# Three unsorted experts, the last gate/up products ahead of the last down products, and a later read of half the scattered rows

## The chip, the cores and the metric

The kernel runs on one core of one Trainium2 chip, as one launch. The metric is the device time in microseconds (us) of one execution. Engines are named as the profile names them: PE is TensorE (PEld its weight loads), DVE is VectorE, ACT is ScalarE, POOL is GpSimd, SP is SyncE, which here only issues transfers. Each engine works through its own queue in order.

## The reference

Two blocks follow each other on 512 tokens of width 1024, in float32. The first has two layers of latent attention with convolution branches. The second has dilated and forgetting attention and then a mixture of 32 experts; only the experts and the last norm are touched here.

```python
group_logits = xt @ w_rg + b_rg                  # 4 groups: the best one is taken
expert_logits = (xt @ w_re + b_re)               # 8 experts in it: the best two are taken
expert_id = g_idx * EXPERTS_PER_GROUP + top_i    # two experts for each of 512 tokens
for e in range(N_EXPERTS):
    he = silu(xt @ w_gate[e]) * (xt @ w_up[e])   # 1024 -> 256
    y = y + combine[:, e:e + 1] * (he @ w_down[e])   # 256 -> 1024
x = x + y
return _rmsnorm(x, final_norm)
```

So there are 1024 pairs of a token and an expert, and 3 MiB of weights for each expert: 2 MiB of gate and up, 1 MiB of down.

## The kernel before, in words

The experts are worked off one after the other. `second_out` and `route_tile` compute the normed tokens, write them to DRAM (`h2d`), and find for each pair its expert and its rank in that expert. `tables_of` turns that into lists of token rows.

The first AH = 5 experts are taken in their natural order, with a block of 128 rows each. The other 27 are sorted by their number of rows (`sort_experts`), so that each place in the order has a fixed block size: `TIERS` gives the first three places of the sorted ones 128 rows, the next two 96, then 64, then 32. The order of work is the string `SEQ`: f stands for the next sorted expert with over 64 rows, m for one with 64, s for one with 32. What doesn't fit into a block goes to extra blocks (`route_extra`, and the loop in `overflow` at the end, which runs as often as there are such blocks). The addresses of a sorted expert's weights come from registers of SP, loaded at L1960 out of the sorted order.

Each expert goes through these steps. `gather` fetches its token rows with an indirect transfer (L1810). `ex_turn` transposes them on PE (`pturn`). `gu` forms the gate and up products (`pgu`): L1827 for blocks over 64 rows, L1838 for small ones, which `fold` then turns and sums (`pfold`, `ef`). `ex_act` forms the gated activation (`eh`). The down products follow in one of two ways. A block over 64 rows has `pye` (L1866), is scaled, and `scatter` writes its rows into a buffer in DRAM (`yd`, one row for each pair) with an indirect transfer. Small blocks go two by two through `pair`: `pyf` (L1887), split in two float32r parts (L1894, L1896), and when 128 rows are together, `ex_add` spreads them over all tokens with a selecting product (`psel`) and adds them to `xk` (L1916). `back` reads the scattered rows (`yb`, L2045) and adds them to `xk` (L2048).

`step(e)` issues the loads ahead (`load`: gate and up of expert e + 5, down of e + 3), the gate/up products of e + 1, the down products of e, the turn of e + 2, the gather of e + 4, some waiting adds, and the fold of e + 1. PE's order is that of the code (`manual_schedule`); a planner orders the other engines' work within the dependences. Gate and up weights lie in a ring of 16 tiles of 512 KB (`eraw`) and four more (`wraw`, for every fifth expert); the reads of scattered rows (`yb`) take tiles of the same ring. Down weights have four places (`wh`, `wl`). All their loads, the reads of `yb` and the writes of the output are in SP's queue. Before the sort, `route_end` issues gate and up of experts 2 to 4 (0 and 1 come earlier), and the down weights of the first three; the fourth's need no sorted order either.

`finish` goes over the four row tiles: the last adds, a square with its sum on ACT (L1928), a root by ten small DVE operations (`rsq`, L231 to L240) for the tiles that `FT` names, the scaling (L1936) and the write of the output (L1937).

Of the kernel before, what the change touches and what calls it, by code (L numbers as in the profile page):

```python
# [10 lines left out]
F32 = mybir.dt.float32  # L11
# [4 lines left out]
OP = mybir.AluOpType  # L16
# [8 lines left out]
NE = 32  # L25
# [4 lines left out]
UNIT = 1040  # L30
PTC = 2
PS2 = (3, 2, 2)
FT = ((0, 2, 1), (2, 4, 3))
HB = 2


# [49 lines left out]
FF = (0.3, 0.2, 0.3)  # L86
PTB = 3
FA, FB = 1.2, 2.4
AH = 5
WH = 3  # L90
TIERS = ((3, 128), (5, 96), (15, 64), (32, 32))
NX = 16
SX = 10
SB = 3
YB = 6
R3 = 0
EL = 3
SO = ((0, 0, 0, 1, 1, 1, 0, 2, 2, 2, 1, 0), (3, 0, 3, 1, 3, 2, 3, 1, 2, 3, 2, 3))
RB = 22
SEQ = "ssfmmfssfmmfssfmmssmmssmmss"  # L100
BE = (lambda nc: nc.vector, lambda nc: nc.vector)
LWP = 8
SQ = "n0 n1 n2 v m2 t0 m2 t1 m2 t2 m2 c0 h00 s2 b04 h10 m2 b04 h20 m2 b14 m4 c1 h01 b14 s2"
# [7 lines left out]
class K:  # L111
# [1741 lines left out]
    def ex_act(self, p, mp):  # L1853

        nc = self.nc
        h = mp.tile([128, 2, 128], F32, name="eh", tag="eh", bufs=3)[:, :, :p.shape[3]]
        nc.scalar.activation(h, p[:, 0], AF.Tanh, scale=0.5)
        nc.vector.scalar_tensor_tensor(h, h, 1.0, p[:, 0], op0=OP.add, op1=OP.mult)
        nc.vector.tensor_tensor(h, p[:, 1], h, op=OP.mult)
        return h  # L1860
# [57 lines left out]
    def finish(self, add):  # L1918
# [5 lines left out]
        for t in range(4):  # L1924
# [4 lines left out]
            os.append(o)  # L1929
            for a, b, at in FT:  # L1930
                if at != t:
# [7 lines left out]
    def moe(self):  # L1939
        nc, I, sp, tc = self.nc, self.I, self.sp, self.tc  # L1940
        xk = self.xk
        mp = self.pool("moe")
# [4 lines left out]
        U, Dn, X, Hs, at = dict(enumerate(self.ahead)), dict(enumerate(self.wd)), {}, {}, {}  # L1947
# [6 lines left out]
        def w_of(i, e):  # L1954
            e = cols[e]
            if e < AH:
                return ws[i][e]
            if e not in at:
                j = e - AH
                at[e] = nc.values_load(self.order[0:1, j:j + 1], engines=[mybir.EngineType.SP], min_val=AH, max_val=NE - 1)  # L1960
            return ws[i][bass.ds(at[e], 1)].rearrange("o a b -> (o a) b")
# [2 lines left out]
            return a[:, cols[e]:cols[e] + 1]  # L1964

        def load(e):
            if e + AH < NE:
                U[e + AH] = self.ex_load(e + AH, w_of(0, e + AH), w_of(1, e + AH))
            if e + WH < NE:
                Dn[e + WH] = self.ex_wd(w_of(2, e + WH))  # L1970

# [4 lines left out]
        def turn(e):  # L1976
            if e < NE:
                X[e] = self.ex_turn(xgs[e % 2], mp, cap[e], e < 2)
# [6 lines left out]
        nc.gpsimd.iota(self.io512, pattern=[[1, 512]], base=0, channel_multiplier=0, allow_small_or_imprecise_dtypes=True)  # L1985
        with tc.issue_after(self.tabled.ins):
            self.sort_experts(mp)
        G = {}

        def gu(e):  # L1990
            if cap[e] > 64:
                Hs[e] = self.ex_gu(U[e], X[e], mp)
            else:
                G[e] = self.ex_half(U[e], X[e], mp, cap[e])

        def fold(e):
            if cap[e] <= 64:
                Hs[e] = self.ex_fold(G[e], mp, cap[e])

# [6 lines left out]
            sc.append(st)  # L2006


        nm, ns = 5, 3
        by = mp.tile([128, 2, nm + ns], F32, name="by")  # L2010

        def rows_by():
            for x, a in enumerate((self.tok, self.wsl)):
                for i in range(2):
                    nc.vector.tensor_copy(by[64 * i:64 * i + 64, x, :nm], a[:64, SX + i:SX + 2 * nm:2])
                for i in range(4):
                    nc.vector.tensor_copy(by[32 * i:32 * i + 32, x, nm:], a[:32, SX + 2 * nm + i:NE:4])

# [19 lines left out]
        B = {}  # L2038

        def back(t):  # L2040

            if t < 4:
                for k in range(2):
                    y = B[t, k] = self.eraw("yb")
                    nc.sync.dma_start(y, self.yd[k * 512 + t * 128:k * 512 + t * 128 + 128, :])  # L2045
            for k in range(2):
                if t:
                    BE[k](nc).tensor_tensor(xk[:, t - 1, :], xk[:, t - 1, :], B[t - 1, k], op=OP.add)  # L2048

        gu(0)  # L2050
        turn(1)
# [3 lines left out]
        waiting, full = [], None  # L2055

        def add(n):

            for x in waiting[:n]:
                self.ex_add(*x)  # L2060
            del waiting[:n]

        def step(e):
            nonlocal full
            load(e)
            if e + 1 < NE:
                gu(e + 1)
            full = None
            if cap[e] > 64:
                scatter(e)  # L2070
            elif cap[:e + 1].count(cap[e]) % 2 == 0:
                full = pair(e)
            turn(e + 2)
            gather(e + 4)
            add(2 if cap[min(e + 1, NE - 1)] > 32 else 1)
            if e + 1 < NE:
                fold(e + 1)
            if e == 1:
                self.route_extra(mp)
                rows_by()  # L2080
            if RB <= e <= RB + 4:
                back(e - RB)
            if full and e + 1 < NE:
                waiting.extend(full + (t,) for t in range(4))

        for e in range(3):
            step(e)
        with tc.manual_schedule(engines={mybir.EngineType.PE}):
            for e in range(3, NE):
                step(e)  # L2090
            add(4)
        self.finish(lambda t: self.ex_add(*full, t))
        self.overflow(mp, xgs[0])
        mp.release()
        self.rp.release()
# [70 lines left out]
```

## Time and profile before

| | us |
|---|---|
| median of 3 runs | 1437.74 (1432.52 to 1438.69) |
| the profiled execution | 1439.8 |
| its span, first to last instruction | 1437.7 |
| PE busy in the span | 1315.5 (92%) |
| DVE busy | 951.7 (66%) |
| ACT busy | 610.1 (42%) |
| POOL busy | 313.4 (22%) |

The mean transfer rate over the span is 171 GB/s. Busy shares are means over stages of different kinds, so the rows below look at the last 340 us alone. In the table by stretches, "DMA share" is the mean busy share of the 16 DMA engines and "PEclk" the granted clock of TensorE, 1.00 being 2.4 GHz and 0.50 being 1.2 GHz. In a timeline, brackets give the idle time of the engine before an instruction and what ended it; instructions in DMA queues (SPq) are issues, not landings.

### The profile page before, as it was taken

What the parts mean: (1) busy time and instruction counts of PE and PEld (TensorE: products, weight loads), DVE (VectorE), ACT (ScalarE), POOL (GpSimd) and SP (SyncE); (2) the same over time, 40 slices, a digit from 0 to 9 for tenths busy, and PEclk for the clock granted to TensorE, in tenths of its full rate; (3) what the DMA queues carried; (4) which work ended last, traced back from release to release, by engine and by line L of the source; (5) the groups of instructions that cost most, each with busy time, mean ns of one, the idle gap of its engine ahead of it and who ended that gap; (6) DMA issues with size and microseconds to landing.
All of it is one profiled execution on the core that took longest, in us unless ns stands there. A gap on an engine that the chain in (4) does not pass through costs nothing. (4 is left out here: it accounts for less than half of the span.)

```text
span 1437.7 us, 22499 instructions
## 1 busy us (share of the span) xinstructions
PE 1315.5 (92%) x8030; PEld 1044.9 (73%) x8030; DVE 951.7 (66%) x2123; ACT 610.1 (42%) x1195; POOL 313.4 (22%) x414
## 2 busy tenths in 40 slices
PE   4999999989989999799999999999997999999873
PEld 3888788877868788678877787887776877675441
DVE  5789997666633789997683646666667443444555
ACT  4543264545531564266573336767553111112111
POOL 5332033322220333143231201111111121111100
PEclk9999999999999999999999999999997999999987
DMA  9643364444132435434233455224545699999971
GB/s 346 150 137 103 100 169 124 129 137 144 63 123 73 116 108 156 125 87 116 69 120 131 151 177 132 77 72 138 171 174 190 222 303 359 378 369 386 389 286 59
DMA packets 167317, 246.45 MB, mean 171 GB/s; under 512 B 47267, under 2 KB 103289, under 8 KB 167205
## 3 DMA queue, kind: packets, MB, share of 16 engines
q1 hardware_dynamic: 161116, 234.95, 49.7%
q0 software_dynamic: 5408, 7.93, 2.1%
q10 hardware_dynamic: 680, 2.13, 0.4%
q8 instruction: 64, 1.05, 0.3%
q14 instruction: 49, 0.39, 0.1%
HBM read 221.74 MB, written 33.33 MB: 177 GB/s over the span
## 5 line engine op out<-in xcount | busy, mean ns | idle before, releaser
L183 DVE TENSOR_TENSOR wlo<-wraw,whi 128x1024 fp32r<-128x1024 f32 (+3 forms) x98 | 118.2, 1212 | 59.3 <-ACT whi L182 58.7
L182 ACT ACTIVATE whi<-wraw 128x1024 fp32r<-128x1024 f32 (+3 forms) x98 | 100.6, 1036 | 102.0 <-PE pout L221 42.7
L219 PE MATMUL pcm<-hTh,whi 128*128 128x256 f32 (+1 forms) x288 | 102.9, 357 | 9.3 <-DVE oa L529 4.3
L569 DVE SCALAR_TENSOR_TENSOR za<-zp,vec,za 128x783 f32<-128x783 f32 (+1 forms) x120 | 108.8, 914 | 0.5
L921 POOL TENSOR_SCALAR P<-P,ll 128x768 f32<-128x768 f32 (+1 forms) x80 | 73.4, 922 | 159.8 <-DVE ll L920 144.9
L221 PE MATMUL pcm<-hTh,wlo 128*128 128x256 f32 (+1 forms) x288 | 99.1, 344 | 0.1
L220 PE MATMUL pcm<-hTl,whi 128*128 128x256 f32 (+1 forms) x288 | 98.6, 342 | 0.0
L183 DVE TENSOR_TENSOR PTl<-pPT,PTh 128x512 fp32r<-128x512 f32 x104 | 70.3, 684 | 28.2 <-ACT PTh L182 27.8
L182 ACT ACTIVATE PTh<-pPT 128x512 fp32r<-128x512 f32 x104 | 60.6, 595 | 47.6 <-PE pPT L934 43.4
L919 ACT ACTIVATE P<-pS,nm 128x768 f32<-128x768 f32 (+1 forms) x80 | 64.9, 814 | 37.4 <-DVE nm L917 31.1
L1810 POOL DMA_INDIRECT xg<-h2d,tok x32 | 31.5, 984 | 209.2 <-PE pturn L1794 131.2
L1416 POOL TENSOR_SCALAR P<-P,l 128x384 f32<-128x384 f32 (+1 forms) x64 | 33.2, 532 | 184.7 <-DVE l L1415 167.6
L917 DVE TENSOR_REDUCE nm<-pS 128x1 f32<-128x768 f32 (+1 forms) x80 | 66.0, 843 | 10.9 <-PE pS L221 10.2
L219 PEld LDWEIGHTS pcm<-hTh,whi 128*128 128x128 f32 x288 | 55.2, 192 | 17.5 <-DVE oa L529 4.9
L219 PE MATMUL pcm<-hT0h,whi 128*128 128x512 f32 x144 | 59.3, 412 | 7.7 <-DVE oa L529 5.8
L934 PE MATMUL pPT<-ident,P 128*128 128x128 f32 x416 | 63.3, 281 | 0.9 <-DVE PTl L183 0.4
L1827 PE MATMUL pgu<-exT,eraw 128*128 128x128 f32 x512 | 61.8, 281 | 0.0
L1827 PEld LDWEIGHTS pgu<-exT,eraw 128*128 128x128 f32 x512 | 60.3, 197 | 1.1 <-DVE exT L1805 0.6
L221 PEld LDWEIGHTS pcm<-hTh,wlo 128*128 128x128 f32 x288 | 55.1, 191 | 6.8 <-DVE wlo L183 0.8
L966 POOL TENSOR_TENSOR oa<-oa,ot 64x256 f32<-64x256 f32 x40 | 37.4, 936 | 102.6 <-DVE ot L965 99.3
L220 PEld LDWEIGHTS pcm<-hTl,whi 128*128 128x128 f32 x288 | 55.3, 192 | 5.1 <-issue 0.5
L220 PE MATMUL pcm<-hT0l,whi 128*128 128x512 f32 x144 | 58.4, 406 | 0.0
(552 smaller groups left out, 3681.6 us busy)
## 6 DMA issues: line engine op xcount, KB each, us to landing
wraw<-in_w_in_dram SPq DMA_DIRECT2D x56, 512.0 KB
eraw<-in_w_expert_gate_dram SPq DMA_DIRECT2D x52, 512.0 KB
eraw<-in_w_expert_up_dram SPq DMA_DIRECT2D x52, 512.0 KB
wraw<-in_w_mod_dram SPq DMA_DIRECT2D x48, 512.0 KB
wl<-in_w_expert_down_dram SPq DMA_DIRECT2D x32, 512.0 KB
wh<-in_w_expert_down_dram SPq DMA_DIRECT2D x32, 512.0 KB
wraw<-in_w_out_dram SPq DMA_DIRECT2D x24, 512.0 KB
wraw<-in_w_expert_gate_dram SPq DMA_DIRECT2D x12, 512.0 KB
```

What stands on the lines that cost most here:

```text
L182: nc.scalar.activation(hi, src, AF.Copy)
L183: return (eng or nc.vector).tensor_tensor(lo, src, hi.bitcast(F32), op=OP.subtract)
L219: mm(out, lhs[0], rhs[0], start=start, stop=False)
L220: mm(out, lhs[0], rhs[1], start=False, stop=False)
L221: mm(out, lhs[1], rhs[0], start=False, stop=stop)
L569: nc.vector.scalar_tensor_tensor(a[:, :nz], z[:, k:k + nz], cfw[:, i, k:k + 1], a[:, :nz], op0=OP.mult, op1=OP.add)
L917: nc.vector.tensor_reduce(nm, S, axis=AX.X, op=OP.max, negate=True)
L919: nc.scalar.activation(P, S, AF.Exp, bias=nm, accum_out=l)
L921: nc.gpsimd.tensor_scalar(P, P, l, 0.5, op0=OP.mult, op1=OP.mult)
L934: nc.tensor.transpose(p[:, jj, i * 128:(i + 1) * 128], Ps[i][:, (j + jj) * 128:(j + jj + 1) * 128], self.ident)
L966: nc.gpsimd.tensor_tensor(o, o, t, op=OP.mult)
L1827: self.last = self.nc.tensor.matmul(p[:, s, c, :], gu[2 * s + k // 4][:, k % 4, c * 128:(c + 1) * 128], x[:, k, :], start=(k == 0), stop=( ...
```

## The change: what it does

- AH goes from 5 to 3: three unsorted experts, 29 sorted ones. The depth of the loads ahead stays at five (LA), so gate and up of the fourth and fifth expert are now loaded after the sort. The tiers become three of 128, two of 96, eight of 64 and sixteen of 32 among the sorted ones: 8 experts are scattered where 10 were, and there are 8 experts with 64 rows where 10 were, and 16 with 32 where 12 were.
- The gated activation has two buffers for blocks over 32 rows and four for those of 32, in place of three for all.
- `route_extra` moves from step 1 to step 15.
- The reads of scattered rows for the first two row tiles come at steps 20 and 21, with their adds a step later. Those for the last two are issued after the last down weights, and their adds stand in `finish`.
- Steps run to 27 only. Then come the gate/up products of the last three experts with their folds and the waiting adds, and after them the last two pairs of down products.
- `FT` names one root over all four row tiles, after the last one, in place of one for each two.

```diff
-FT = ((0, 2, 1), (2, 4, 3))
+FT = ((0, 4, 3),)
...
-AH = 5
+AH = 3
+LA = 5
 WH = 3
-TIERS = ((3, 128), (5, 96), (15, 64), (32, 32))
+TIERS = ((3, 128), (5, 96), (13, 64), (32, 32))
 NX = 16
-SX = 10
+SX = 8
...
-RB = 22
-SEQ = "ssfmmfssfmmfssfmmssmmssmmss"
+RB = 20
+END = 28
+SEQ = "ssfmmfssfmmfssfssmmssssmmssss"
...
-        h = mp.tile([128, 2, 128], F32, name="eh", tag="eh", bufs=3)[:, :, :p.shape[3]]
+        n = p.shape[3]
+        h = mp.tile([128, 2, 128 if n > 32 else n], F32, name="eh", tag=f"eh{n > 32}", bufs=2 if n > 32 else 4)[:, :, :n]
...
-            if e + AH < NE:
-                U[e + AH] = self.ex_load(e + AH, w_of(0, e + AH), w_of(1, e + AH))
+            if e + LA < NE:
+                U[e + LA] = self.ex_load(e + LA, w_of(0, e + LA), w_of(1, e + LA))
...
             self.sort_experts(mp)
+        for e in range(AH, LA):
+            U[e] = self.ex_load(e, w_of(0, e), w_of(1, e))
...
-        nm, ns = 5, 3
+        nm, ns = 4, 4
...
-            if t < 4:
-                for k in range(2):
-                    y = B[t, k] = self.eraw("yb")
-                    nc.sync.dma_start(y, self.yd[k * 512 + t * 128:k * 512 + t * 128 + 128, :])
             for k in range(2):
-                if t:
-                    BE[k](nc).tensor_tensor(xk[:, t - 1, :], xk[:, t - 1, :], B[t - 1, k], op=OP.add)
+                y = B[t, k] = self.eraw("yb")
+                nc.sync.dma_start(y, self.yd[k * 512 + t * 128:k * 512 + t * 128 + 128, :])
+
+        def back_add(t):
+            for k in range(2):
+                BE[k](nc).tensor_tensor(xk[:, t, :], xk[:, t, :], B[t, k], op=OP.add)
...
             if e == 1:
+                rows_by()
+            if e == 15:
                 self.route_extra(mp)
-                rows_by()
-            if RB <= e <= RB + 4:
+            if RB <= e <= RB + 1:
                 back(e - RB)
+            if RB < e <= RB + 2:
+                back_add(e - RB - 1)
...
-            for e in range(3, NE):
+            for e in range(3, END):
                 step(e)
+            load(END)
+            for t in (2, 3):
+                back(t)
+            for e in range(END + 1, NE):
+                gu(e)
+                turn(e + 1)
+                add(1)
+                fold(e)
             add(4)
-        self.finish(lambda t: self.ex_add(*full, t))
+            pair(NE - 3)
+            full = pair(NE - 1)
+
+        def last(t):
+            if t > 1:
+                back_add(t)
+            self.ex_add(*full, t)
+
+        self.finish(last)
```

## Rows read from the trace of the kernel before

**Rows 1.** The page: the span in 40 equal slices, GB/s moved by DMA

```profile
GB/s 346 150 137 103 100 169 124 129 137 144 63 123 73 116 108 156 125 87 116 69 120 131 151 177 132 77 72 138 171 174 190 222 303 359 378 369 386 389 286 59
```

**Rows 2.** Stretches: length, busy us (instructions) by engine, PEclk, DMA share, GB/s

```profile
core 0: us, PE busy (x) PEld busy (x) DVE busy (x) ACT busy (x) POOL busy (x), PEclk, DMA share, GB/s
1100.00:1116.00 16.00, 7.51 (x34) 7.18 (x35) 13.98 (x69) 3.39 (x7) 2.92 (x2) 0.50 0.52 191
...
1120.00:1135.00 15.00, 15.00 (x134) 14.76 (x133) 6.03 (x30) 2.86 (x10) 1.00 (x1) 1.00 0.65 214
1135.00:1200.00 65.00, 62.53 (x474) 47.08 (x474) 28.05 (x83) 8.12 (x16) 11.92 (x12) 1.00 0.91 303
1185.00:1195.00 10.00, 9.57 (x92) 8.69 (x88) 2.59 (x6) 1.02 (x3) 1.54 (x2) 1.00 1.03 361
1200.00:1360.00 160.00, 152.99 (x1206) 98.45 (x1200) 72.89 (x136) 28.37 (x54) 23.68 (x25) 1.00 1.02 380
1360.00:1385.00 25.00, 17.93 (x113) 9.70 (x110) 14.38 (x22) 3.13 (x6) 0.90 (x1) 0.86 1.02 405
1385.00:1394.00 9.00, 4.91 (x34) 3.46 (x38) 6.86 (x10) 0.31 (x1) 0.00 (x0) 0.81 0.68 272
```

**Rows 3.** Timeline of SP's queue around the sort: start us, us of issuing, transfer

```profile
1095.04 0.44 SPq L1781 DMA_DIRECT2D wl<-in_w_expert_down_dram  x1
1120.41 1.24 SPq L1766 DMA_DIRECT2D eraw<-in_w_expert_gate_dram  x2
```

**Rows 4.** Line 1960, SP's register loads: ns min/median/max, first and last start us

```profile
L1960 SPq TENSOR_LOAD <-order x27: 260/269/470, 1113.9 to 1155.9; - x27
```

**Rows 5.** Timeline of DVE in the sort: start us, us, operation

```profile
1108.54 0.92 DVE L1657 TENSOR_TENSOR sx<-key 128x729 f32<-128x729 f32 x1
...
1113.70 0.16 DVE L1670 CAST order<-order 1x27 int32<-1x27 f32 x1
```

**Rows 6.** Timeline of PE: a large block, small blocks, the last pairs

```profile
1127.27 7.39 PE L1827 MATMUL pgu<-exT,eraw 128*128 128x128 f32 x64
1134.49 1.02 PE L1866 MATMUL pye<-wh,eh 128*128 128x512 f32 x2
...
1137.93 1.04 PE L1794 MATMUL pturn<-ident,xg 128*128 128x128 f32 x8
...
1336.57 3.67 PE L1838 MATMUL pgu<-eraw,exT 128*64 128x256 f32 x32
1340.17 0.68 PE L1794 MATMUL pturn<-ident,xg 32*128 32x32 f32 x8
...
1342.74 0.60 PE L1848 MATMUL pfold<-ident,eg 128*128 128x128 f32 x4
1343.27 1.93 PE L1838 MATMUL pgu<-eraw,exT 128*32 128x256 f32 x32
...
1394.56 1.08 PE L1887 MATMUL pyf<-wh,eh 128*64 128x512 f32 x4
...
1406.17 1.44 PE L1887 MATMUL pyf<-wl,eh 128*32 128x512 f32 x7
```

**Rows 7.** Timeline of SP's queue: the last weight tile

```profile
1385.23 0.33 SPq L1781 DMA_DIRECT2D wl<-in_w_expert_down_dram  x1
```

**Rows 8.** Timeline of DVE from the third read of scattered rows to the end

```profile
1370.73 1.23 DVE L2048 TENSOR_TENSOR xk<-xk,yb 128x1024 f32<-128x1024 f32 x1 [5.25 <-DMA yb<-yd]
...
1409.63 1.52 DVE L1896 SCALAR_TENSOR_TENSOR ys<-pyf,by,ys 64x512 fp32r<-64x512 f32 x2
1411.18 6.07 DVE L1916 TENSOR_TENSOR xk<-psel,xk 128x512 f32<-128x512 f32 x10
...
1418.03 0.68 DVE L1916 TENSOR_TENSOR xk<-psel,xk 128x512 f32<-128x512 f32 x1
...
1422.59 0.16 DVE L232 TENSOR_SCALAR rt<-rv 128x2 int32<-128x2 int32 x1
...
1424.37 2.48 DVE L1936 SCALAR_TENSOR_TENSOR fo<-xk,fs,fin 128x1024 f32<-128x1024 f32 x2
```

**Rows 9.** Timeline of ACT: the last square

```profile
1418.75 1.06 ACT L1928 ACTIVATE fo<-xk 128x1024 f32<-128x1024 f32 x1 [0.31 <-DVE xk L1916]
```

## The prediction

> **What bounds the kernel now.** I read the page first: its slices of DMA traffic [rows 1] are light and uneven for most of the span and near 380 GB/s in the last quarter, so the expert part, which alone the change touches, has another bound than the rest. Then the busy table by stretches of that part [rows 2]. From 1100 to 1116 us, while the routing is worked out, the DMA engines have half a load; from 1120 to 1135 they move 214 GB/s and to 1200 303 GB/s; from 1200 to 1385 they are full (share 1.02) at 380 to 405 GB/s, and at 1394 the last weights are in. TensorE is busy nearly throughout to 1360 (153.0 of 160 us) and only 17.9 of 25 us after that. So it is paced by TensorE at first, by both for a while, and by the stream of weights at the end.
>
> The queue's own rows say why the stream starts slowly: nothing is issued between 1095.04 and 1120.41 [rows 3]. Five experts' gate/up weights and four down weights are in by then, and the next load needs a buffer that the first gate/up products give back. The register loads that a sorted expert needs begin at 1113.9 and take 0.47 us at most [rows 4]; they follow VectorE's sort, whose order is written at 1113.86 [rows 5].
>
> After the stream comes the tail. At 1394.56 the second-last pair's down products start, and the last pair's end at 1407.61 [rows 6]; the last weight tile was issued at 1385.23 [rows 7]. VectorE then finishes the parts at 1411.15, the adds at 1418.71, and the scaled rows at 1426.85 [rows 8], with the last square on ScalarE from 1418.75 [rows 9]. The span ends 10.8 us later, with the output's landing and the program's end.
>
> **The stream, part by part.** One load is 512 KB, 0.524 MB. From 1120 to 1394 the windows add up to 214x15 + 303x65 + 380x160 + 405x25 + 272x9 = 96.3 MB [rows 2]. Of these 27 experts' gate/up are 56.6 MB, 28 down weights 29.4, eight reads of scattered rows 4.2; 6.1 are gathers and scatters.
>
> With three unsorted experts, gate/up of the fourth and fifth (4.2 MB) and the fourth's down weights (1.05 MB) need the sorted order. They move from before the sort, where they cost nothing, into the stream: 5.24 MB, 13.7 us at 382 GB/s (the last two full stretches: 70.9 MB in 185 us). Against that, four of the eight reads (2.1 MB, 5.5 us) go behind the last weights, and scatters fall: the reference's router gives the 32 experts 4 to 115 rows, so eight scattered experts have 539 rows where ten had 605, 0.27 MB less. The blocks stay large enough (the 14th-largest sorted expert has 25 rows, the limit there is 32), so no overflow block runs. Bytes up to the last weights: 96.3 + 5.24 - 2.1 - 0.27 = 99.2 MB.
>
> Start: the sort grows from 27x27 to 29x29, 15% on five passes of 0.92 us, +0.7 us [rows 5]; with the register load [rows 4] the first new load is issued at about 1115.3, and I let data flow from 1118, a couple of us later. It has free buffers, so the hole in [rows 3] closes by 5 us and the stream no longer waits for the first products. Will it then be full? The buffers after that are released by gate/up products: an unsorted expert costs TensorE 7.2 us, its down products 3.4 and the turn 1.0 [rows 6], 11.6 in all, longer than the 8.7 us its 3.33 MB take. But only three such come now before two of the smallest; five came before. For example, the stream wants the second set's buffer after 7.3 MB, at 1138, and its products end at 1134.5; it wants the third's 3.3 MB later, at 1147.5, and that product, 12.6 us behind the second's, ends at 1147. So release and wish fall together within a few us.
>
> At what rate? Full stretches show 361 GB/s (1185 to 1195) and 380 to 405 later [rows 2]. I take 361 to 1200 and 383 after: 82 us x 0.361 = 29.6 MB, and 69.6 MB / 0.383 = 182 us, so the last weights are in at 1382 where they were at 1394. Ends: 1376 (382 from 1116 on) and 1398 (286 GB/s to 1200, as the 22.9 MB in 80 us of before). I stay nearer the full row, because what held the early loads back was a buffer, and those now have one.
>
> The Trainium skill, "DMA: Bandwidth & Descriptors", section "Where 436 GB/s comes from", says that for HBM to SBUF the memory's per-core limit of about 358 GB/s binds. The trace speaks against it: 405 GB/s over 25 us [rows 2]. By it the weights would be in at 1118 + 99.2/0.358 = 1395, an estimate from that page.
>
> **TensorE.** Two 128-row experts and two 64-row ones become four 32-row ones. Removed: 2 x 11.6 us and 2 x (3.7 gate/up + 0.6 fold + 0.8 turn + 1.8, half of a pair's four rows like that at 1394.56); added: 4 x (1.9 + 0.6 + 0.7 + about 1.1) [rows 6]. That is 23.2 + 13.8 - 17.2 = 20 us less; the select products stay at eight sets. Before, TensorE reached 1343 just behind the weights; now it is there some 20 us of work earlier and the stream alone ends the stage. The 20 us are therefore cover and not gain; without them the stream's 12 us could not show.
>
> The tables for the extra blocks move from step 1 to step 15, some 60 small VectorE operations, to a place where TensorE has that cover: 0, at worst a few us of cover. Two buffers instead of three for the large gated activations: tanh of an expert behind a 64-row pair waits for that pair's down products; on ScalarE only the pair's own parts queue behind it, and TensorE has a turn and the next gate/up (2.5 us) before it wants the result. 0, at most 1 us twice. Pair and select order otherwise: 0.
>
> **The tail.** Count from the arrival T of the last weights, at 1394 before, with 43.7 us to go. Now gate/up of the last three are done when their weights land, 8.2 us (three down weights) ahead of T, and the second-last pair as well, so only the last pair's second half is left: 1.0 us (the last seven recorded products of the old end took 1.44). The old path needed 13.6 us there. Parts: ScalarE, then VectorE 1.52; 3.5 us before, with adds in the way; I take 3.0, and 0.5 to the first select result. Then VectorE: eight adds at 0.61 are 4.9 [rows 8], and four adds of the scattered rows at 1.23 are another 4.9, which stood earlier before. Their data come 5.5 us after T and some 3 us of drain, while VectorE is at the first adds. Last square 1.06 [rows 9], with the read-out of its sum 1.3, root 2.0 (the second one: 1422.59 to 1424.37 and a first step of 0.2), four scalings 5.0, end 10.8. Sum: 1.0 + 3.0 + 0.5 + 9.8 + 1.3 + 2.0 + 5.0 + 10.8 = 33.4.
>
> Two parts bring little by this. The single root: the first of the two was hidden by the last square, so what it saves is given back by a square that nothing hides; 0, between -2 and +1.3. Reading half the rows late: 5.5 us off the stream, 4.9 us onto VectorE. Should SyncE's order put these reads ahead after all, T is 1387.5 and the adds are out of the tail: the same end. What goes besides is the wait of 5.2 us for such a read at the head of VectorE's queue at 1370.73 [rows 8], with pyf parts and select products behind it.
>
> Sum: 1382 + 33.4 = 1415.4; 1 us more for matmuls of the tail at the lower clock (0.81 to 0.86 in the last stretches [rows 2], with TensorE waiting). Span 1416. The profiled execution of before took 1439.8 with a span of 1437.7, and the median is 1437.74, 2.1 below; 21.7 us off that median is **1416**.
>
> **Rivals.**
> (a) The stream runs at the lower full rate, 361, all the way: T = 1118 + 275 = 1393, end 1426. For: the 1185 row, full with 361; against: 185 us at 383 after it. The rule named above gives nearly this.
> (b) The early stream stays at 286 GB/s, since gathers, scatters and released buffers shape it and not the late start: T = 1398, end 1431.
> (c) The same place, worse, and slower than before: a load issued only when a product gives its buffer back, at the 214 GB/s of 1120 to 1135, to 1200. 17.5 MB by then, 81.7 MB / 0.383 = 213 us: T = 1413, end 1447. It is slower by 0.5% when the early rate is under 222 GB/s. For: the row shows that rate; against: two more experts' buffers are free at that time.
> (d) VectorE's queue has an add of scattered rows ahead of the last pairs' parts, as at 1370.73. The last read lands at about T + 8.5; then an add, parts, the last pair, parts and eight adds follow: 1423; with the last folds behind it too, 1428.
> (e) TensorE idles so long between the last weights that its clock is at 1.2 GHz for the last 8 us before T: the gate/up, fold, selects and pair of that time, about 8 us, become 15 or 16, and the end 1424. For: clock 0.86 in the last full stretch, with 17.9 of 25 us busy. The Trainium skill, "TensorE: Matmul & The Clock Gate", Part 1, says that the default state is the throttled one and activity releases it, which speaks against an end in which TensorE waits more. The trace agrees so far as those two stretches are the only ones below 1.00 after 1120.
>
> **Chances.** Forecast (1403 to 1424) 0.53; (a) 0.10; (b) 0.13; (c) 0.07; (d) 0.09; (e) 0.08. A difference under 0.5% (7.2 us) can't be told from none here. Faster: forecast, (a), (d), (e) and 0.05 of (b): 0.85. Same: 0.08 of (b), 0.02 of (c): 0.10. Slower: 0.05. The range for 8 in 10 runs from 1403 (T = 1376, and 6 us for yb adds that fall into gaps) to 1431, where (b) lies.
>
> **What would show it.** After: first load of a sorted expert issued near 1115; DMA share 0.95 or more from 1120; the last down weights in at about 1382; gate/up L1838 of the last three before the last two pairs; no wait for yb on VectorE above 2 us; one root; the span ending 33 us after T. It is wrong if the share from 1120 to 1200 is still under 0.9, or if the time from T to the end is above 40 us.

## The result: 1415.99 us, and the profile after

The changed kernel took 1415.99 us (median of 4 runs, 1411.91 to 1417.19) where the kernel before took 1436.2 beside it; the ratio is 0.9853, 95% interval 0.9829 to 0.9878. The forecast was 1416. The profiled execution took 1415.46 us with a span of 1413.6. Medians in this text leave out two slow executions, one of the kernel before (4449.08 us) and one of the run without tables (2522.74 us). The agreement of the totals says little by itself, so the steps are checked one by one below.

A first look at the page, the DMA rate in 40 slices, which answers to [rows 1]:

```profile
GB/s 343 159 134 109 97 150 156 132 109 172 60 134 64 98 128 146 136 55 160 31 134 148 112 192 152 87 73 139 137 73 168 258 383 383 371 373 325 395 407 83
```

The full rate begins one slice earlier, and there is a new dip, 325, in the fifth full slice. The stretches show both (columns as in [rows 2]):

```profile
1100.00:1116.00 16.00, 9.40 (x52) 9.29 (x53) 14.80 (x58) 2.48 (x10) 4.25 (x3) 0.56 0.47 149
1116.00:1120.00 4.00, 4.00 (x38) 4.00 (x37) 2.15 (x16) 0.61 (x2) 0.00 (x0) 1.00 1.00 378
1120.00:1135.00 15.00, 15.00 (x106) 12.35 (x105) 6.54 (x17) 3.02 (x10) 1.78 (x2) 1.00 1.03 399
1135.00:1200.00 65.00, 63.49 (x514) 43.29 (x516) 19.61 (x39) 10.65 (x20) 12.62 (x14) 1.00 1.01 381
1200.00:1360.00 160.00, 144.63 (x1141) 94.37 (x1135) 86.12 (x192) 26.65 (x52) 19.92 (x22) 0.93 0.99 371
1260.00:1280.00 20.00, 17.87 (x109) 15.11 (x109) 8.44 (x41) 1.75 (x3) 0.95 (x1) 0.74 0.78 291
1360.00:1376.00 16.00, 16.00 (x162) 9.93 (x159) 9.72 (x21) 3.93 (x8) 0.91 (x1) 1.00 1.03 408
1376.00:1385.00 9.00, 7.90 (x50) 3.47 (x48) 7.23 (x13) 2.99 (x5) 0.00 (x0) 1.00 0.48 191
```

From 1120 to 1135 the rate is 399 GB/s where it was 214, and to 1200 it is 381 where it was 303: the hole of [rows 3] ends earlier, and the stream is full behind it. SP's queue around the sort (start, us of issuing, transfer):

```profile
1088.26 0.44 SPq L1783 DMA_DIRECT2D wl<-in_w_expert_down_dram  x1
1110.14 0.94 SPq L1768 DMA_DIRECT2D eraw<-in_w_expert_gate_dram  x2
```

Absolute times mislead here. The sort's first product starts at 1102.54 in the profile of before and at 1097.15 in this one. Ahead of it only weight loads were taken away, and most of the difference (4.9 us) was already there at 460 us, long before those loads; in the thirteen profiles with any part of the change this product starts between 1095.0 and 1102.7. So from here on times are counted from that product. By it the first sorted load is issued 13.0 us in, where it was 17.9. The hole itself is still there, since the queue waits for the sorted order. What is gone is the wait behind it: before, the order was written at 1113.86 [rows 5] and the load issued 6.6 us later, when the first gate/up products gave a buffer back; now the order is written at 1108.77 and the load issued 1.4 us later.

The end on TensorE (start, us, then what ended the idle time before it):

```profile
1331.88 1.04 PE L1890 MATMUL pyf<-wh,eh 128*32 128x512 f32 x2
1340.93 1.07 PE L1890 MATMUL pyf<-wh,eh 128*32 128x512 f32 x3 [8.00 <-DMA wh<-in_w_expert_down_dram]
...
1373.26 1.93 PE L1840 MATMUL pgu<-eraw,exT 128*32 128x256 f32 x32
...
1378.53 1.07 PE L1890 MATMUL pyf<-wh,eh 128*32 128x512 f32 x8
...
1381.13 1.04 PE L1890 MATMUL pyf<-wl,eh 128*32 128x512 f32 x8
```

The last three gate/up products do stand ahead of the last pairs, whose products now run without a wait to 1382.2. But TensorE works from 1341 to there with one gap of 0.4 us, and that one is for VectorE: it waits for no weights at the end, so it is a little behind them. VectorE's tail, which answers to [rows 8]:

```profile
1383.66 1.54 DVE L1899 SCALAR_TENSOR_TENSOR ys<-pyf,by,ys 64x512 fp32r<-64x512 f32 x2 [0.19 <-ACT ys L1897]
1385.23 2.48 DVE L1919 TENSOR_TENSOR xk<-psel,xk 128x512 f32<-128x512 f32 x4
1387.63 4.62 DVE L2053 TENSOR_TENSOR xk<-xk,yb 128x1024 f32<-128x1024 f32 x4
1392.17 2.48 DVE L1919 TENSOR_TENSOR xk<-psel,xk 128x512 f32<-128x512 f32 x4
1395.86 0.17 DVE L233 TENSOR_SCALAR rv<-fs 128x4 f32<-128x4 f32 x1 [1.22 <-ACTq L2129]
...
1397.86 4.87 DVE L1939 SCALAR_TENSOR_TENSOR fo<-xk,fs,fin 128x1024 f32<-128x1024 f32 x4
```

None of these adds waits for the scattered rows, there is one root, and the span ends 10.9 us after the last scaling.

### The profile page after: what moved, and what is told of

The parts are those of the page before. It is cut to its first block, busy times and chain, and to the rows that moved or that the text cites. A ratio compares the mean times of both kernels' runs of the same rounds, so it can differ in the third digit from the quotient of the medians.

```text
span 1413.6 us, 22394 instructions
## 1 busy us (share of the span) xinstructions
PE 1291.6 (91%) x7974; PEld 1026.3 (73%) x7974; DVE 947.3 (67%) x2113; ACT 611.2 (43%) x1197; POOL 311.0 (22%) x412
## 3 DMA queue, kind: packets, MB, share of 16 engines
q8 instruction: 64, 1.05, 0.3%
## 5 line engine op out<-in xcount | busy, mean ns | idle before, releaser
L1812 POOL DMA_INDIRECT xg<-h2d,tok x32 | 31.5, 983 | 219.9 <-PE pturn L1796 165.1
L223 PE MATMUL pcm<-hT0h,wlo 128*128 128x512 f32 x144 | 58.2, 404 | 0.0
L1829 PE MATMUL pgu<-exT,eraw 128*128 128x128 f32 x448 | 55.8, 289 | 0.0
## 6 DMA issues: line engine op xcount, KB each, us to landing
eraw<-in_w_expert_gate_dram SPq DMA_DIRECT2D x52, 512.0 KB, 10.1
wraw<-in_w_expert_gate_dram SPq DMA_DIRECT2D x12, 512.0 KB, 13.1
```

The lines of the kernel that those rows point to most:

```text
L223: mm(out, lhs[1], rhs[0], start=False, stop=stop)
L1829: self.last = self.nc.tensor.matmul(p[:, s, c, :], gu[2 * s + k // 4][:, k % 4, c * 128:(c + 1) * 128], x[:, k, :], start=(k == 0), stop=( ...
```

## The experiments

Theory at the start: the stream of weights moved as forecast, and what is missing in the tail is TensorE's lateness, caused by the tables for the extra blocks at step 15. The timeline of TensorE at that place in the changed kernel:

```profile
1256.70 0.60 PE L1850 MATMUL pfold<-ident,eg 128*128 128x128 f32 x4
1261.66 1.04 PE L1733 MATMUL pposx<-obx,oo 128*128 128x32 f32 x4 [4.36 <-DVE obx L1732]
1262.85 3.67 PE L1733 MATMUL pposx<-obx,oo 128*128 128x32 f32 x12 [0.16 <-DVE obx L1732]
1266.33 9.69 PE L1829 MATMUL pgu<-exT,eraw 128*128 128x128 f32 x64
```

TensorE waits 4.4 us for VectorE, the granted clock of 1260 to 1280 is 0.74, and the same 64 products that take 7.4 us elsewhere [rows 6] take 9.7. SP stands behind it: no load is issued from 1267.9 to 1277.1, until the pair behind those products gives its down-weight places back. (In the second profile of the same kernel, further down, the hole is smaller: share 0.92 from 1260 to 1280.)

All runs in one table: median and ratio to the kernel before, run beside it on the same chip, and from each one's profile the issue of the last weight tile, the end of the last pair's products and the end of the span, all in us from the sort's first product.

| kernel | median us | ratio (95%) | last tile issued | last pair ends | span ends |
|---|---|---|---|---|---|
| before | | | 282.7 | 305.1 | 335.2 |
| changed | 1415.99 | 0.9853 (0.9829 to 0.9878) | 271.3 | 285.0 | 316.5 |
| changed, again | 1416.21 | 0.9838 (0.9823 to 0.9853) | 270.4 | 282.6 | 314.1 |
| tables at step 1 | 1417.95 | 0.9858 (0.9839 to 0.9876) | 273.3 | 287.5 | 319.0 |
| rows read early | 1418.41 | 0.9871 (0.9852 to 0.9891) | 275.0 | 292.6 | 319.6 |
| old order at the end | 1421.50 | 0.9894 (0.9875 to 0.9913) | 271.6 | 290.6 | 323.8 |
| two roots | 1414.89 | 0.9858 (0.9837 to 0.9878) | 268.5 | 282.0 | 313.2 |
| the tail alone | 1431.56 | 0.9951 (0.9935 to 0.9967) | 275.4 | 290.0 | 325.7 |
| the experts alone | 1426.82 | 0.9922 (0.9902 to 0.9941) | 276.9 | 295.0 | 323.8 |
| tables in step 25 | 1416.00 | 0.9862 (0.9843 to 0.9881) | 267.5 | 284.8 | 316.3 |
| no tables | 1417.17 | 0.9856 (0.9833 to 0.9879) | 268.2 | 282.0 | 313.9 |
| gate/up ahead | 1417.81 | 0.9869 (0.9847 to 0.9891) | 272.1 | 284.1 | 315.6 |
| both | 1414.54 | 0.9837 (0.9813 to 0.9861) | 269.8 | 282.4 | 313.8 |
| half of gate/up | 1415.29 | 0.9826 (0.9803 to 0.9848) | 269.5 | 280.7 | 312.6 |

**Tables at step 1.**

```diff
             if e == 1:
                 rows_by()
-            if e == 15:
                 self.route_extra(mp)
```

> The changed kernel with one edit: the tables for the extra blocks are built at step 1 again, not at step 15. Theory: at step 15 TensorE's order is that of the code, so the eight products of these tables wait for VectorE's chain; TensorE starts the next gate/up 9 us late and at half clock (1266 instead of 1257 us, 9.7 instead of 7.3 us long), the down weights' buffers come free late and the DMA engines fall to 207 GB/s for 10 us, 5 to 6 us of stream. At step 1 the planner puts the products between gate/up products. Expected: 5 to 7 us less from the first count product of the routing (pcnt) to the end of the span, 310 us instead of 316.5; no stretch from 1150 to 1360 under 340 GB/s. Rival: the stream or TensorE has cover there, as the prediction had it: 316.5 within 1.5.

1417.95 us, and 319.0 by the stage where 310 was forecast: no gain. The hole did not vanish, it moved to where the tables now are (1160 to 1180: share 0.81):

```profile
1160.00:1180.00 20.00, 19.22 (x165) 13.68 (x158) 5.82 (x12) 3.46 (x7) 1.99 (x2) 0.96 0.81 276
1260.00:1280.00 20.00, 19.68 (x188) 14.67 (x186) 11.46 (x23) 2.87 (x6) 3.74 (x4) 1.00 1.03 384
```

**The reads of scattered rows early, all four.**

```diff
-            if RB <= e <= RB + 1:
+            if RB <= e <= RB + 3:
                 back(e - RB)
-            if RB < e <= RB + 2:
+            if RB < e <= RB + 4:
                 back_add(e - RB - 1)
...
-            for t in (2, 3):
-                back(t)
...
-            if t > 1:
-                back_add(t)
```

> The changed kernel with one edit: all four pairs of reads of scattered rows ahead of the last weights (steps 20 to 23), their adds at steps 21 to 24, none in the last part. Prediction's arithmetic: weights 5.5 us later, 4.9 us of adds out of the tail: from pcnt to the end 317, within 1.5. Theory B, that TensorE and not the last weights ends the stage (it is 5 to 7 us behind them in the changed kernel): later weights are partly hidden, 313 to 315. Rival C: the adds wait at the head of VectorE's queue for their reads as in the kernel before (5.2 us there) and hold parts and folds: 320 to 323.

The stage is 3.1 us longer and the ratio 0.0018 higher (2.6 us, inside the intervals). The last tile is issued 3.7 us later, and the adds are out of the tail: 27.0 us from the last pair to the end, where the changed kernel needs 31.5. The 319.6 lies between the first forecast (317, within 1.5) and rival C (320 to 323). What the profile shows for it is the old wait, back at the head of VectorE's queue, and later TensorE's select products, which wait for VectorE and run at a low clock (0.66 from 1360 to 1370):

```profile
1341.87 1.23 DVE L2053 TENSOR_TENSOR xk<-xk,yb 128x1024 f32<-128x1024 f32 x1 [6.34 <-DMA yb<-yd]
```

```profile
1361.46 1.22 PE L1917 MATMUL psel<-ys,sel 128*128 128x512 f32 x2 [4.50 <-DVE xk L1919]
```

**The old order at the end** (the late reads stay behind the last weights).

```diff
             load(e)
+            if e == END:
+                back(2)
+                back(3)
...
-            for e in range(3, END):
+            for e in range(3, NE):
                 step(e)
-            load(END)
-            for t in (2, 3):
-                back(t)
-            for e in range(END + 1, NE):
-                gu(e)
-                turn(e + 1)
-                add(1)
-                fold(e)
             add(4)
-            pair(NE - 3)
-            full = pair(NE - 1)
```

> The changed kernel with one edit: the last steps in the old order (gate/up of one expert, then the pair before it, then its fold), reads of the last scattered rows still behind the last weights. The prediction counted 12.6 us for having gate/up and the second-last pair done ahead: by that, pcnt to end goes from 316.5 to about 325 or more. Rival: in the changed kernel TensorE runs without a gap from 1341 to 1382 and does the same products in either order; then only the waits from fold to pair are exposed, and it is 317 to 320.

5.9 us slower by the ratios, 7.3 by the stage: 323.8, between the forecast (325 or more) and the rival (317 to 320). The profile shows what the new order takes away: the second-last pair waits for its weights, and the fold and gate/up products behind it run at a low clock (1.05 and 2.36 us, where the changed kernel has 0.60 and 1.93).

```profile
1370.50 0.63 PE L1890 MATMUL pyf<-wh,eh 128*32 128x512 f32 x3 [2.79 <-DMA wh<-in_w_expert_down_dram]
...
1376.41 1.05 PE L1850 MATMUL pfold<-ident,eg 128*128 128x128 f32 x4
1377.39 2.36 PE L1840 MATMUL pgu<-eraw,exT 128*32 128x256 f32 x32
```

**Two roots.**

```diff
-FT = ((0, 4, 3),)
+FT = ((0, 2, 1), (2, 4, 3))
```

> The changed kernel with one edit: two roots, as before, one for each two row tiles. The prediction gave the single root 0, between -2 and +1.3: pcnt to end 316.5, within 1.5. Rival: the first root finds room in the 1.2 us wait for the last square and the second costs 1.8 us more, 318.5; or the first two outputs start 2 to 4 us earlier and the end comes earlier, 315.

0.9858 beside 0.9853: nothing, as forecast. From the last pair's end to the end of the span it takes 31.2 us, the changed kernel 31.5. Its profile also gave a warning. Its instructions are those of the changed kernel up to the last pair, yet its last pair ends at 282.0 where the other's ends at 285.0. Single profiles of this stage differ by 3 us, so smaller differences between rows of the table decide nothing.

**The tail alone**, on the old set of experts (AH = 5 with its tiers, order and places, the first reads at step 22), tables at step 1. The two kinds of buffers for the gated activation stay as in the change, here and in the next run; no run undoes them alone.

```diff
-AH = 3
+AH = 5
...
-            if e == 15:
                 self.route_extra(mp)
...
-            pair(NE - 3)
+            both = pair(NE - 3)
             full = pair(NE - 1)
+            for t in range(4):
+                self.ex_add(*both, t)
```

> Five unsorted experts, tiers, SEQ and early tables as before; of the change only the new end: gate/up of the last three ahead of the last two pairs, half the scattered rows read behind the last weights, one root (the last 64-row set is added right after the last pair). Prediction's sums: 5.5 us off the stream and 10.3 off the tail: from the first count product (pcnt) to the end of the span 335.2 - 15.8 = 319. Rival: TensorE, with 20 us more of products than in the changed kernel, is late at the end anyway and the order is worth the 7 us that the order experiment showed, the late reads 3: 325.

**The experts alone**: the changed kernel with the old order at the end, all rows read early, two roots and the tables at step 1, each as in the diffs above.

> Three unsorted experts, the new tiers and SEQ (tables for extra blocks at step 1), the old end: old order, all rows read ahead of the last weights, two roots. Prediction's sums: of the 12 us of the stream 6.5 are without the late reads, so pcnt to end is 335.2 - 6.5 = 329. Rival: the parts' measured worth (order 7, late reads 3, roots 0) taken from the changed kernel's 316.5 leaves 326.5.

The tail alone gives 7.0 us (0.49%), the experts alone 11.2 (0.78%), together 1.27% against the 1.47 to 1.62% of the whole. The last tile is issued 7.3 and 5.8 us earlier than before, 13.1 together, against 11.4 to 12.3. So the two halves add up about, within what the intervals allow; neither gives the other's gain back.

Their sizes are not those of the forecasts. By the stage the tail alone ends at 325.7, where the prediction's sums gave 319 and the rival 325. The experts alone end at 323.8, where the sums gave 329 and the rival 326.5. So the tail is worth 9.5 us of the stage and not 15.8, the experts 11.4 and not 6.5. Two things stand behind this. First, in the tail alone eight more adds follow the last pair than in the changed kernel, since the old second-last pair fills 128 rows by itself: from the last pair to the end it takes 35.7 us, the changed kernel 31.5, so some 4 us of the shortfall are the experiment's own. Second, the old end itself is shorter behind the new experts: from the last tile's issue to the end of the span the experts alone take 46.9 us, the kernel before 52.5. What in that end is shorter no run separates.

**Tables in step 25**, between its gate/up products and its pair, where TensorE waits for down weights anyway.

```diff
             if e + 1 < NE:
                 gu(e + 1)
+            if e == 25:
+                self.route_extra(mp)
...
-            if e == 15:
-                self.route_extra(mp)
```

> The changed kernel with the tables for extra blocks built in step 25, behind that step's gate/up and ahead of its pair, where TensorE waits 8 us for down weights. Moving them to step 1 gave nothing and left a hole of the same size in the stream at 1160 to 1180 (276 GB/s), so the theory now is: up to step 20 the stream waits on places for down weights that the pairs free, any 5 us of TensorE there cost 5 us of stream, and only the last steps have cover. Expected: no stretch under 340 GB/s from 1120 to 1370, and pcnt to end 311 (5 less). Rival: TensorE ends the stage after its own last products, so a delay at step 25 goes through: 316 to 320.

**No tables**: the lists that they fill are set to zero instead.

```diff
             if e == 15:
-                self.route_extra(mp)
+                for a, z in ((self.tok, 0), (self.scat, 0), (self.wsl, 0.0)):
+                    nc.gpsimd.memset(a[:, 32:], z)
+                nc.gpsimd.memset(self.exinfo, 0)
```

> The changed kernel without the tables for extra blocks (they are set to zero; the loop over extra blocks runs no block with these inputs). It measures what these tables cost in all, wherever they stand. If the stream's hole at 1270 to 1280 and TensorE's 9 us there are theirs: pcnt to end 309 to 311, 5.5 to 7 less. If the hole belongs to the places of the down weights and would come anyway: 315 to 317.

In both the hole is gone; the first stretch is of the run with the tables in step 25, the second of the one without:

```profile
1260.00:1280.00 20.00, 18.86 (x167) 11.23 (x167) 9.59 (x19) 4.14 (x8) 3.75 (x4) 1.00 1.03 376
```

```profile
1260.00:1280.00 20.00, 19.68 (x155) 13.76 (x154) 9.33 (x18) 3.70 (x7) 1.87 (x2) 1.00 1.02 368
```

Yet the times are 1416.0 and 1417.2. My theory, that the tables' hole is what the tail lacks, fell. The last tile is issued 3 to 4 us earlier, and with the tables in step 25 the last pair does not follow: it ends 17.3 us after that issue, in the changed kernel 13.7. There TensorE waits 6.0 us for VectorE at the tables' products, and the pair behind them runs at a low clock (1.94 us for eight products that take 1.04 elsewhere); the end at 316.3 is the rival's. (Without tables the last pair ends 3 us earlier, no more than the two-roots profile does by chance, and the stage at 313.9, between the two forecasts.) New theory: TensorE's work behind its last long wait (8.0 us, at 1340.9) sets the end.

**Gate/up ahead**: the last 64-row expert's turn, the fold before it and its gate/up products ahead of that wait.

```diff
...
+            if early:                  # in step 25
+                turn(e + 2)
+                fold(e + 1)
+                gu(e + 2)
+                done.update((e + 2, -e))
             full = None
...
```

> The changed kernel, but the last 64-row expert's turn, the fold before it and its gate/up products (1.1 + 0.6 + 3.7 us) stand ahead of the pair that TensorE waits 8 us for (1332.9 to 1340.9 in the changed kernel), instead of behind it. Theory (the end is set by TensorE's work behind that wait, 41 us without a gap, with the last weights in some 5 us earlier than it gets to them): the wait shrinks by those 5 us, what stands behind it too, and the end comes 3 to 5 us earlier, until the last weights bind again: 312 to 314 us from the first pcnt product to the end of the span where the changed kernel has 316.5, and 1411 to 1413 as a time. Rival (the stream sets the end, and TensorE's lateness is only what the stream left): no change, 316 us and 1416. Second rival: the gate/up weights of that expert land no earlier than the down weights waited for, so TensorE waits for them instead: no change or 1 us slower, with the wait shown at the gate/up products.

No gain. The wait of 8.0 us did not shrink by the 5.4 us of work moved, it split in two (2.3 and 4.7), and part of it stands at the moved products themselves, as the second rival had it; here is TensorE:

```profile
1339.39 5.36 PE L1840 MATMUL pgu<-eraw,exT 128*64 128x256 f32 x32 [2.33 <-DMA eraw<-in_w_expert_gate_dram]
...
1360.77 1.09 PE L1890 MATMUL pyf<-wh,eh 128*64 128x512 f32 x1 [4.69 <-DMA wh<-in_w_expert_down_dram]
```

The stream runs at 406 to 411 GB/s through all of this: the wait is the stream's, wherever it is put.

**Both**: that, and the tables in two parts (VectorE's sums at step 20, one-hots and products in step 25).

```diff
         V.tensor_scalar(bi, bi, 1.0, None, op0=OP.subtract)
+        yield
...
-            if e == 15:
-                self.route_extra(mp)
+            if e == 20:
+                extra.append(self.route_extra(mp))
+                next(extra[0])
...
                 gu(e + 2)
+                next(extra[0], None)
```

> As the run before it, and the tables for the extra blocks are worked out in two parts: VectorE's sums at step 20, the one-hots and the eight products at step 25, behind the gate/up products that were moved ahead and still ahead of the pair, inside the wait for down weights. Theory: no stretch of 20 us before 1360 with the DMA share under 0.95, the last weights in some 5 us earlier than in the changed kernel, and with TensorE's work ahead of the wait both limits move: 309 to 312 us from the first pcnt product to the end, 1408 to 1411 as a time. Rival (the hole in the stream never mattered at this place): the same as the run before it within 1 us. Second rival: the products wait for VectorE for more than the pair's wait (6 us in the run with the tables whole in step 25): 2 to 3 us slower than the run before it.

1414.54 us, ratio 0.9837, 313.8 by the stage: not the 1408 to 1411 and the 309 to 312 that the theory wanted, and not apart from the unchanged kernel's 0.9838. No version here is shown to beat the changed kernel.

**Half of gate/up**: the last five experts' gate/up products go over half of the depth.

```diff
-    def ex_half(self, gu, x, mp, n):
+    def ex_half(self, gu, x, mp, n, K=8):
...
-            for k in range(8):
+            for k in range(K):
...
-                G[e] = self.ex_half(U[e], X[e], mp, cap[e])
+                G[e] = self.ex_half(U[e], X[e], mp, cap[e], 4 if e > 26 else 8)
```

> The changed kernel, but gate/up of its last five experts multiplies only half of the depth (16 products instead of 32 each; the other half of the sum is left out). Every load, fold, turn, select and down product stays. This takes 5.7 us (half of 3.7 and of four times 1.9) from TensorE behind its last wait, and nothing from the stream. Theory (that work without a gap sets the end, and the last weights are in some 6 us ahead of their use): the last pair's products end 4 to 6 us earlier, 279 to 281 us after the first pcnt product where the changed kernel has 285.1, and the end comes at 311 to 313, 1410 to 1412 as a time, a ratio near 0.981. Rival (the stream sets the end): the products of the last pair wait for the last down weights by as much as was taken out, and the time is that of the unchanged one, 1416, a ratio near 0.985.

**The changed kernel again**, with no edit.

> The changed kernel once more, with no edit, beside the run before it and as a measure of how far two profiles of one program stand apart: the run with two roots has the same instructions up to the last square, and its last pair ended 282.0 us after the first pcnt product where this one's ended at 285.1. Theory: that is the spread of single executions, so this one lies between 281 and 286, with its wait for down weights between 6 and 9 us, and the time is 1414 to 1418, a ratio of 0.984 to 0.987. Rival: single profiles repeat to half a microsecond in this stretch, and the 3 us were the two roots'; then it is 285 again.

The unchanged kernel's second profile lies where its theory put it: the last pair ends at 282.6, the wait for down weights is 7.0 us, the time 1416.21. So 5.7 us less work brought 0.9 us in the medians (0.0012 in the ratios, inside the intervals). At the last pair's end it brought 4.3 us beside the first profile and 1.9 beside the second. By the first the forecast came true (280.7 in 279 to 281, the end at 312.6 in 311 to 313), by the time it did not (1415.29, not 1410 to 1412). With two profiles 2.4 us apart this doesn't decide on the second theory; what it excludes is a gain of 4 to 6 us in the time. In the run with half of the products the last pair now waits for weights; the profile puts this down to the last tile, which would so land 10.1 us after its issue at 1372.22 (TensorE's weight loads):

```profile
1382.30 0.15 PEld L1890 LDWEIGHTS pyf<-wl,eh 128*32 128x32 f32 x6 [0.96 <-DMA wl<-in_w_expert_down_dram]
```

In the unchanged kernel's second profile the same loads stand at 1381.98 and wait for nothing, 11.1 us after the issue (1370.88):

```profile
1381.98 0.13 PEld L1890 LDWEIGHTS pyf<-wl,eh 128*32 128x32 f32 x4 [0.30 <-issue]
```

If a tile lands as late there, TensorE is about 1 us behind the stream; in the first profile (issue 1368.45, loads 1381.13) it is 12.7 - 10.1 = 2.6 us behind. By this one landing the two limits stand that close together, which would explain why taking away the tables' hole, or the wait, or 5.7 us of TensorE's work alone moved the time by nothing that can be measured. The kernel with both moved would have had to show 1408 to 1411 if only these two held the end; why it gained no more than 1 or 2 us, with its last tile issued at 269.8, is the part that I did not settle. From 1320 on it ran at 382 to 403 GB/s with share 1.02, so I see little left to gain in the last 60 us by order.

## Why the prediction was right

The forecast change was 21.7 us: 12 earlier for the last weights, 10.3 less behind them, 1 back for the clock (21.3; the span, 1416.4 by the terms, was rounded to 1416). In the two profiles of the changed kernel the last tile is issued 11.4 and 12.3 us earlier than before, and from that issue to the end it is 45.2 and 43.6 us where it was 52.5 [rows 7]: 7.3 and 8.9 less, where 9.3 net was forecast. Together that is 18.7 and 21.1; the medians make 20.2 and 22.8. The stream's half of the sum holds. In what each part of the change is worth two errors cancelled, and that the total came out so close is in part luck: the prediction took the new end for 15.8 us (5.5 of stream and 10.3 of tail) and the new experts for 6.5. Alone, by one profile each, they brought 9.5 (some 4 more without the adds that the changed kernel doesn't have) and 11.4; the ratios say 7.0 and 11.2. By steps:

- **Hole at the sort**: right. It ends 4.9 us earlier (forecast 5), the wait for a buffer behind the order is gone, and the share from 1120 to 1200 is 1.01 to 1.03. Rivals (b) and (c) are excluded by 399 and 381 GB/s in the rows above.
- **Rate**: too low to 1200, 361 forecast against 381 to 399; too high behind it, 383 against 371 to 1360, with the dip; 408 after 1360. The errors cancel, and (a) is excluded. The Trainium skill's limit of about 358 GB/s ("DMA: Bandwidth & Descriptors", "Where 436 GB/s comes from") does not hold here, with one core running: 408 over 16 us.
- **Tables at step 15 at "0, at worst a few us of cover"**: wrong as to the place, right in the sum. They cost TensorE the 4.4 us of waiting, 2.3 us of low clock, and SP 9 us without a load. Without them or with them elsewhere the time is the same within 2 us.
- **The 20 us of TensorE, "cover and not gain"**: the size is about right (TensorE's busy time from the sort's first product on fell by 17.8 us, from 283.0 to 265.2, and by 21.3 in the second profile), the use is not. As cover it is less than I took, since 8 us of it go in one wait at 1340.9, and TensorE comes out of that wait at the low clock; without it, in the tail alone, the last pair ends 14.6 us after the last issue instead of 12.1 to 13.7, about what two profiles differ by. But some of it is gain: behind the new experts the old end is 5.6 us shorter (46.9 for 52.5, from the last issue to the end), which the prediction put at nothing.
- **Second half of the last pair, 1.0**: mis-sized. By the same mark as in the forecast (the last weights 8.8 us after their last issue, as 1385.23 and 1394 in [rows 2, 7]) it measured 4.9 and 3.3. Of this 1.3 would be that the last tile lands 10.1 us after its issue, as in the run where a wait shows it; beside the 1.0 itself the rest is TensorE, 1 to 2.6 us behind. So from the arrival of the last weights by that mark to the end it is 36.4 and 34.8 us, where 33 was forecast and above 40 was named as a sign of being wrong.
- **Order at the end, 12.6**: too large. Undoing it costs 5.9 us by the ratios and 7.3 by the stage (8.1 and 9.7 beside the second record of the changed kernel), half to three quarters. The old path of 13.6 us in [rows 6] contained VectorE's backlog and a clock of 0.81 to 0.86 [rows 2]. Here is TensorE in the kernel before, waiting for VectorE's adds shortly before that path, which then runs without a wait for weights:

```profile
1389.09 2.86 PE L1914 MATMUL psel<-ys,sel 128*128 128x512 f32 x6 [4.50 <-DVE xk L1916]
```

This wait of 4.5 us is there in the three kernels that read all the rows early (before, rows read early, the experts alone), and from 1300 on no such wait is above 0.3 us in the others. So part of the 12.6 goes with the late reads; in the run with the old order, which keeps them, the last pair ends 18.9 us after the last issue where before it was 22.4.
- **Parts, adds, square, root, scalings, end**: 3.0, 9.4, 1.2, 2.0, 4.9 and 10.9 measured against 3.0, 10.3, 1.3, 2.0, 5.0 and 10.8.
- **One root, 0**: right. **Late reads, about 0 and the wait of 5.2 us gone**: the wait went, and undoing this costs some 3 us, with the wait back; that is less than the intervals tell apart. Rival (d), VectorE stalled by the late reads, did not come: the adds follow with no wait. Rival (e) came at another place: the clock is 1.00 from 1360 to 1385, so the 1 us for it in the tail wasn't needed there, but it is low after the wait at 1340.9. VectorE waited once for a read of the first two tiles, above the 2 us that I had set:

```profile
1333.14 2.58 DVE L2053 TENSOR_TENSOR xk<-xk,yb 128x1024 f32<-128x1024 f32 x2 [2.97 <-DMA yb<-yd]
```

## What to carry to other kernels

Work out the stream's last arrival and the compute engine's last start as two separate times: here they lay within a few us of each other, and none of the edits that were meant to shorten the end changed the time by more than the intervals. Price the halves of a change each by a run of its own: a total that agrees can hide terms that are wrong by several us each way. A step moved "under cover" has to be priced at the queue that stands behind it (here SP, held by a buffer that the delayed product frees), and its hole may still cost nothing. Before reading differences of 3 us between two profiles, profile the same kernel twice.

## What the runs showed of the hardware

The transfers reached 406 to 411 GB/s for 30 us on end in the run with gate/up ahead (1336 to 1366), when nearly all that moved was weight tiles of 512 KB, against 351 (rows read early, 1200 to 1220, share 1.02) to 376 in stretches of equal share with more gathers and with scatters among them (no run tests that they are the cause): a share of 1.0 is no one rate. With the queue full a tile landed 10.1 us after its issue by the one wait that shows it, an estimate of 8 tiles in flight at 408 GB/s. TensorE came out of the 8.0 us wait at the lower of its two levels, 1.2 GHz, and four select products took 2.07 us where they usually take 1.21; the stretch behind the wait, in the changed kernel:

```profile
1341.00:1345.00 4.00, 4.00 (x19) 1.00 (x20) 0.00 (x0) 0.37 (x1) 0.00 (x0) 0.50 1.03 409
```
